# Linear attention: head sums of the diagonal products taken with the products as the moving side on four column blocks, then transposed

## The chip, the cores and the metric

The kernel runs on one core of one Trainium2 chip. The metric is the time of one execution in microseconds of device time. TensorE (PE) multiplies, with its weight loads shown apart as PEld; VectorE (DVE), ScalarE (ACT) and GpSimd (POOL) work elementwise; SyncE (SP) issues the DMAs. Each engine runs its own instructions in the order in which the program lists them.

## The reference

Two layers over 2048 latent tokens and 256 context tokens. Each layer normalises and modulates the stream, projects it once, runs three branches (a gated delta rule, a neighbourhood attention, and a gated linear attention, "GLA"), gates them and projects back. The change lies in GLA alone. Per direction, with `g` the running sum of the gates inside a chunk, it computes

```python
diff = bcum[..., :, None, :] - bcum[..., None, :, :]
decay = jnp.where(tril, jnp.exp(jnp.where(tril, diff, 0.0)), 0.0)
amat = jnp.einsum('bhnid,bhnjd,bhnijd->bhnij', q, k, decay)
o_intra = jnp.einsum('bhnij,bhnjv->bhniv', amat, v)
```

for 4 heads of 32 key channels, then adds the part that comes from the state of earlier chunks. Both directions are summed.

## The kernel before

All 2304 tokens are cut into 6 blocks of 384 tokens (`BLK`), each 3 tiles of 128 tokens (`TPB`). `Dense.run` multiplies the stream by a group of projection columns, block by block: for each output, 24 matmuls of line 197 (8 slices of the model width, 3 products of a high and a low part each). After the dense work of block `b` of the first such run of a layer, the program calls `Gla.block(b)` (`after=gla.block`). So twice per run of the kernel, once per layer, there is a stretch in which TensorE has dense work and GLA work side by side. There are 12 GLA blocks; in the first block of the second layer only one tile of three needs scores (`i0 = 2`), so they count as 11.33 full ones.

`Gla.block` holds channels on the partitions (128 = 4 heads x 32) and tokens along the free side. VectorE forms the running sums `B` (lines 432 and 433), and for seven levels `s` = 64, 32, 16, 8, 4, 2, 1 the decayed keys and queries `a` (lines 444 to 449, with ScalarE's exponential on line 448); the last ones of these are what the diagonal products need. GpSimd then multiplies keys and queries elementwise into `qkp` (line 472): four products x = 0 to 3, one for the token with itself and three for its near neighbours. A sum over the 32 channels of each head is a sum over partitions, so TensorE does it: for each product and each tile one matmul with the 128x128 product as the stationary side and 4 columns of a constant (`mats[:, 8]`) as the moving side, into `pD` (line 476). VectorE copies `pD` to `dg` (line 478). `scores` (once per head) multiplies keys and queries of the levels 64 to 4 on small tiles of the array, into `pA` and `pB` (lines 494 and 501); ScalarE copies `pA` to `A` (line 504); VectorE builds `G` from `pB` and `dg` (lines 507 to 511) and puts it into `A` (line 514). `chunk` multiplies `A` with the values (`pO`, line 528), transposes the keys (`pk`, line 537) and forms the change of the state (`pS`, line 543).

All these PSUM tiles (`pr`, `pg`, `pD`, `pA`, `pB`, `pO`, `pk`, `pS`) rotate through 4 buffers of one tag, in the order in which the program allots them. `qkp` x = 1 to 3 lies in the SBUF buffers of tag `rp`, `B` in those of tag `B`. Which ready instruction stands next on an engine is decided when the program is built, by a scheduler that estimates times and prefers what stands earlier in the program; on the chip the order is then fixed.

Of the kernel before, what the change touches and what calls it, by code (L numbers as in the profile page):

```python
# [11 lines left out]
F32 = mybir.dt.float32  # L12
# [15 lines left out]
BLK = 384  # L28
NB = T // BLK
TPB = BLK // 128  # L30
# [305 lines left out]
class Gla:  # L336
# [64 lines left out]
    def block(self, b):  # L401
        e, nc, P = self.e, self.e.nc, self.p
        mats = e.mats
# [27 lines left out]
        B = P.tile([128, 2, BLK], F32, tag="B", name="B")  # L431
# [3 lines left out]
        i0 = max(0, self.first - b * TPB)  # L435
        o = i0 * 128
# [31 lines left out]
        qkp = []  # L468
        for i, (l, r) in enumerate([(qk[:, 0], qk[:, 1])] + [(KQ[s][:, 0], KQ[s][:, 1]) for s in (1, 2, 2)]):
            if i % 2 == 0:  # L470
                qkp.append(P.tile([128, 2, BLK], F32, tag="rp" if i else "ga", name="qkp"))
            nc.gpsimd.tensor_tensor(quad(qkp[-1][:, i % 2]), quad(l), flip(quad(r), i), op=ALU.mult)
        pD = self.ps.tile([128, TPB, 4, 4], F32, tag="ps", name="pD")
        for x in range(4):
            for i in range(i0, TPB):
                nc.tensor.matmul(pD[:, i, x], qkp[x // 2][:, x % 2, i * 128:i * 128 + 128], mats[:, 8, 4 * min(x, 1):4 * min(x, 1) + 4], start=True, stop=True)  # L476
        self.dg = P.tile([128, TPB, 4, 4], F32, tag="dg", name="dg")
        nc.vector.tensor_copy(self.dg[:, i0:], pD[:, i0:])
        A = [self.scores(h, KQ, i0) for h in range(4)]
        for i in range(TPB):  # L480
            self.chunk(b * TPB + i, i, A, E, et[:, i:i + 1], V[:, i])
# [1071 lines left out]
```

## Time and profile before

| what | value |
|---|---|
| median of 3 runs | 3960.82 us (3921.74 to 3962.12) |
| profiled execution | 3949.59 us, its span 3947.8 us |
| TensorE busy | 3618.4 us, 92% |
| VectorE busy | 2455.6 us, 62% |
| ScalarE busy | 1687.4 us, 43% |
| TensorE's mean granted clock | 0.91 |

The span is the time from the first to the last instruction of the profiled execution. Busy times of the engines overlap. A row of a timeline gives the start in us from the span's start, the length in us, the engine, the line, the operation, the tile that is written and those that are read, the shape, and in brackets the idle time of the engine before it and what ended it. A float32 matmul leaves two records (x272 is 136 matmuls). The granted clock has two levels in these rows: 0.5 is 1.2 GHz, 1.0 is 2.4 GHz.

### The profile page before, as it was taken

What the parts mean: (1) busy time and instruction counts of PE and PEld (TensorE: products, weight loads), DVE (VectorE), ACT (ScalarE), POOL (GpSimd) and SP (SyncE); (2) the same over time, 40 slices, a digit from 0 to 9 for tenths busy, and PEclk for the clock granted to TensorE, in tenths of its full rate; (3) what the DMA queues carried; (4) which work ended last, traced back from release to release, by engine and by line L of the source; (5) the groups of instructions that cost most, each with busy time, mean ns of one, the idle gap of its engine ahead of it and who ended that gap; (6) DMA issues with size and microseconds to landing.
All of it is one profiled execution on the core that took longest, in us unless ns stands there. A gap on an engine that the chain in (4) does not pass through costs nothing.

```text
span 3947.8 us, 76664 instructions
## 1 busy us (share of the span) xinstructions
PE 3618.4 (92%) x27262; PEld 3113.5 (79%) x27262; DVE 2455.6 (62%) x6983; ACT 1687.4 (43%) x4587; POOL 682.8 (17%) x1118
## 2 busy tenths in 40 slices
PE   6999999999989999998998999999999899989898
PEld 3787778769977888896776778777899688878787
DVE  4456463668966477446884655427788567653577
ACT  3533233435533455565544333333455235545531
POOL 0221111220102222220002211102102132222100
PEclk8988889999999799999997889899999888879899
DMA  9844325886687777766755444468665977685664
GB/s 294 284 133 141 124 84 167 264 264 198 208 271 227 223 210 208 211 204 213 238 178 172 141 129 137 131 202 246 202 213 193 324 207 213 194 215 171 218 204 125
DMA packets 756085, 787.55 MB, mean 199 GB/s; under 512 B 190206, under 2 KB 665206, under 8 KB 755702
## 3 DMA queue, kind: packets, MB, share of 16 engines
q1 hardware_dynamic: 755702, 782.64, 64.5%
q8 instruction: 216, 3.54, 0.4%
q14 instruction: 167, 1.37, 0.1%
HBM read 548.41 MB, written 234.03 MB: 198 GB/s over the span
## 4 chain that ended last, share of the span: by engine, by line
PE 60%; DMA 18%; DVE 13%; ACT 4%; SPq 2%; issue 2%; POOL 1%; DVEq 0%; ACTq 0%; POOLq 0%
PE p L197 29%; PE py L197 6%; DMA mm<-MS 3%; PE p L1258 3%; DMA gb<-GR 2%; DMA o<-OA 1%; PE pv L1022 1%; PE po L1042 1%; PE pd L1029 1%; DMA kk<-KK 1%; PE p L104 1%; PE pk L1011 1%; PE po L1044 1%; DVE acc L661 1%; PE pD L476 1%
## 5 line engine op out<-in xcount | busy, mean ns | idle before, releaser
L197 PE MATMUL p<-mm,wh 128*128 128x384 f32 (+1 forms) x3648 | 995.8, 352 | 51.9 <-DMA mm<-MS 32.4
L197 PEld LDWEIGHTS p<-mm,wh 128*128 128x128 f32 (+1 forms) x3648 | 661.3, 191 | 123.2 <-DMA mm<-MS 48.1
L197 PE MATMUL p<-mm,wl 128*128 128x384 f32 (+1 forms) x1824 | 630.0, 347 | 0.4 <-DVE wl L189 0.3
L197 PE MATMUL p<-wh,mm 128*128 128x512 f32 (+1 forms) x1696 | 566.5, 407 | 11.4 <-DMA mm<-MS 4.5
L197 PEld LDWEIGHTS p<-wh,mm 128*128 128x128 f32 x1696 | 329.4, 197 | 89.7 <-DMA mm<-MS 9.2
L661 DVE SCALAR_TENSOR_TENSOR acc<-pre,cw,acc 128x384 f32<-128x384 f32 (+1 forms) x576 | 358.3, 640 | 49.8 <-ACT acc L659 43.0
L197 PEld LDWEIGHTS p<-mm,wl 128*128 128x128 f32 (+1 forms) x1824 | 346.5, 190 | 16.1 <-issue 9.7
L197 PE MATMUL p<-wl,mm 128*128 128x512 f32 (+1 forms) x848 | 342.4, 404 | 1.2 <-DVE rst L395 1.0
L197 PEld LDWEIGHTS p<-wl,mm 128*128 128x128 f32 x848 | 167.3, 197 | 36.2 <-issue 2.2
L197 PE MATMUL py<-w,mh 128*128 128x512 f32 x544 | 178.8, 407 | 7.7 <-ACT mh L1380 5.0
L1004 POOL TENSOR_TENSOR kd<-kk,eD 128x256 f32<-128x256 f32 x144 | 89.3, 620 | 453.2 <-DMA kk<-KK 190.0
L1274 DVE SCALAR_TENSOR_TENSOR zt<-zt,p 128x256 f32<-128x256 f32 (+1 forms) x102 | 51.5, 507 | 178.9 <-ACT zt L1273 177.9
L1237 ACT ACTIVATE w<-w,mn 128x696 f32<-128x696 f32 (+2 forms) x136 | 112.8, 830 | 82.8 <-DVE mn L1234 80.0
L651 POOL COPY pre<-pre 128x4 f32<-128x4 f32 x120 | 81.0, 678 | 383.8 <-DVE acc L661 190.9
L925 DVE TENSOR_TENSOR tmp<-M 96x30 f32<-96x30 f32 (+4 forms) x360 | 126.6, 352 | 29.7 <-issue 21.9
L1015 DVE SCALAR_TENSOR_TENSOR R<-pk,neG,kk 128x128 f32<-128x128 f32 x272 | 81.4, 344 | 100.9 <-PE pk L1011 100.0
L865 DVE SCALAR_TENSOR_TENSOR gb<-gb,Gt,mats 128x128 f32<-128x128 f32 x288 | 86.4, 359 | 91.4 <-DMA gb<-GR 88.9
L1258 PE MATMUL p<-v,wl 120*128 120x64 f32 (+1 forms) x960 | 140.5, 285 | 0.0
L926 DVE TENSOR_TENSOR M<-M,tmp 96x30 f32<-96x30 f32 (+4 forms) x360 | 127.3, 354 | 6.3
L1258 PEld LDWEIGHTS p<-v,wl 120*128 120x128 f32 (+1 forms) x960 | 130.6, 204 | 0.7
L186 ACT CAST wh<-raw 128x512 fp32r<-128x512 f32 (+3 forms) x144 | 75.8, 555 | 123.6 <-DMA raw<-in_w_in 105.7
L189 POOL TENSOR_TENSOR mm<-mm 128x384 fp32r<-128x384 f32 x48 | 58.4, 1222 | 398.2 <-ACT mm L186 391.7
(307 smaller groups left out, 8136.1 us busy)
## 6 DMA issues: line engine op xcount, KB each, us to landing
mm<-MS SPq DMA_DIRECT2D x384, 384.0 KB
kk<-KK SPq DMA_DIRECT2D x144, 512.0 KB
MS<-mm SPq DMA_DIRECT2D x96, 384.0 KB
raw<-in_w_in SPq DMA_DIRECT2D x104, 256.0 KB
w<-in_w_mod SPq DMA_DIRECT2D x96, 256.0 KB
M<-m SPq DMA_DIRECT2D x36, 512.0 KB
mm<-M SPq DMA_DIRECT2D x96, 192.0 KB
KK<-kq SPq DMA_DIRECT2D x96, 192.0 KB
```

The source lines that it names most:

```text
L186: eng_hi.copy(hi, src)
L189: eng_lo.tensor_tensor(lo, src, hi.bitcast(F32), op=ALU.subtract)
L197: e.nc.tensor.matmul(p, x(k), y(k), start=n == 0, stop=n == 3 * KD - 1)
L651: nc.gpsimd.tensor_copy(pre[:, 0:4], pre[:, m:m + 4])
L661: nc.vector.scalar_tensor_tensor(acc[:, :n], pre[:, k:k + n], w(kind, k), acc[:, :n], op0=ALU.mult, op1=ALU.add)
L865: nc.vector.scalar_tensor_tensor(E[:, d, h], gb[:, d, h], self.G[:, d, c, h0 + h:h0 + h + 1], e.mats[:, 1 + d], op0=ALU.subtract, op1=ALU.min)
L925: nc.vector.tensor_tensor(tv, col, row, op=ALU.mult)
L926: nc.vector.tensor_tensor(o, o, tv, op=ALU.add)
L1004: nc.gpsimd.tensor_tensor(kd, kv[:, :, 0], self.eD[:, d, c, h0:h0 + 2].unsqueeze(2).to_broadcast([128, 2, 128]), op=ALU.mult)
L1015: nc.vector.scalar_tensor_tensor(R[:, h], pk[:, h], sc(self.neG, h), kv[:, h, 1], op0=ALU.mult, op1=ALU.add)
L1237: nc.scalar.activation(w[:, a, 0:256 + nk], w[:, a, 0:256 + nk], AF.Exp, bias=m[:, a:a + 1], scale=-1.0, accum_out=sm[:, a:a + 1])
L1258: nc.tensor.matmul(p[:, a], l, r, start=j == 0, stop=j == len(parts) - 1)
```

## The change

The four products are no longer the stationary side. The constant, widened to 32 columns of which the first 4 count, is stationary, and the product of a whole block (384 tokens) is the moving side. Each of the four matmuls writes its own 32 partitions of one PSUM tile `pX`, that is, its own block of 32 columns of the array (`tile_position=(0, 32 * x)`). The result has heads on the partitions and tokens along the free side; ScalarE copies it to `dT` (in the SBUF buffer of tag `B`), TensorE transposes `dT` tile by tile into `pD`, which is now 3 x 128 wide, and VectorE copies the 4 columns that count of each 32 to `dg`.

```diff
-        pD = self.ps.tile([128, TPB, 4, 4], F32, tag="ps", name="pD")
+        pX = self.ps.tile([128, BLK], F32, tag="ps", name="pX")
         for x in range(4):
-            for i in range(i0, TPB):
-                nc.tensor.matmul(pD[:, i, x], qkp[x // 2][:, x % 2, i * 128:i * 128 + 128], mats[:, 8, 4 * min(x, 1):4 * min(x, 1) + 4], start=True, stop=True)
+            c = 4 * min(x, 1)
+            nc.tensor.matmul(pX[32 * x:32 * x + 32, o:], mats[:, 8, c:c + 32], qkp[x // 2][:, x % 2, o:], start=True, stop=True, tile_position=(0, 32 * x))
+        dT = P.tile([128, 2, BLK], F32, tag="B", name="dT")[:, 0]
+        nc.scalar.copy(dT[:, o:], pX[:, o:])
+        pD = self.ps.tile([128, TPB, 128], F32, tag="ps", name="pD")
+        for i in range(i0, TPB):
+            nc.tensor.transpose(pD[:, i], dT[:, i * 128:i * 128 + 128], e.ident)
         self.dg = P.tile([128, TPB, 4, 4], F32, tag="dg", name="dg")
-        nc.vector.tensor_copy(self.dg[:, i0:], pD[:, i0:])
+        nc.vector.tensor_copy(self.dg[:, i0:], pD[:, i0:].rearrange("p i (x c) -> p i x c", x=4)[:, :, :, 0:4])
```

Since six lines are added, what was line 494 is line 500 after the change, 501 is 507, 504 is 510. The new lines are 477 (`pX`), 479 (`dT`), 482 (the transposes) and 484 (`dg`).

The order of the instructions changes with it. TensorE before, second block of the first layer, from the middle of the scores: `pD` x9 are the last nine of the twelve sums, `pA` and `pB` the scores.

```order
L501 MATMUL pB<-a 32x32 x40
L494 MATMUL pA<-a 64x64 x2
L494 MATMUL pA<-a 32x32 x4
L501 MATMUL pA<-a 32x32 x4
L494 MATMUL pA<-a 64x64 x2
L494 MATMUL pA<-a 32x32 x4
L501 MATMUL pA<-a 32x32
L476 MATMUL pD<-mats,qkp 128x4 x9
L501 MATMUL pB<-a 32x32 x8
L501 MATMUL pA<-a 32x32 x3
```

Of that block's 216 score matmuls 125 stand ahead of these nine sums and 91 behind them. TensorE after the change, the same block, first at the last three of the four new sums and then at the transposes:

```order
L197 MATMUL p<-mm,wh 128x384
L197 MATMUL p<-mm,wl 128x384
L477 MATMUL pX<-qkp,mats 32x384 x3
L371 MATMUL pt<-ident,r_4563 128x48 x3
L197 MATMUL p<-mm,wh 128x384 x2
L197 MATMUL p<-mm,wl 128x384
```

```order
L197 MATMUL p<-wh,mm 128x512
L197 MATMUL p<-wl,mm 128x512
L197 MATMUL p<-wh,mm 128x512 x2
L482 MATMUL pD<-ident,dT 128x128 x3
L500 MATMUL pA<-a 64x64 x2
L500 MATMUL pA<-a 32x32 x4
L507 MATMUL pA<-a 32x32 x4
L507 MATMUL pB<-a 32x32 x8
```

All 216 score matmuls now stand behind the transposes, in one run without dense work between them. This is so in each of the 12 blocks (in the short one 72, with 4 dense matmuls among them); between the last `pX` and the transposes 12 to 28 dense matmuls stand. Before, 76 to 138 of the 216 stood ahead of the last sums.

VectorE after the change, fourth block of the first layer, from the copy to `dg` on:

```order
L1087 SCALAR_TENSOR_TENSOR nqk<-p,nqk 128x192 x2
L484 COPY dg<-pD 128x48
L513 COPY G<-pB 128x96
L515 COPY_PREDICATED G<-masks,pB 128x96
L517 COPY_PREDICATED G<-masks,dg 128x96 x4
L520 COPY_PREDICATED A<-masks,G 32x3x32 x4
L513 COPY G<-pB 128x96
L515 COPY_PREDICATED G<-masks,pB 128x96
```

Before, the first two operations (`G<-pB`) of two heads stood ahead of the copy to `dg` in this block; now those of all four heads stand behind it.

## Rows read from the trace of the kernel before

**Rows 1.** Page of the profile: span; then busy time and share of each engine.

```profile
span 3947.8 us, 76664 instructions
PE 3618.4 (92%) x27262; PEld 3113.5 (79%) x27262; DVE 2455.6 (62%) x6983; ACT 1687.4 (43%) x4587; POOL 682.8 (17%) x1118
```

**Rows 2.** Page, the chain that ended last: shares of the span by line.

```profile
PE p L197 29%; PE py L197 6%; DMA mm<-MS 3%; PE p L1258 3%; DMA gb<-GR 2%; DMA o<-OA 1%; PE pv L1022 1%; PE po L1042 1%; PE pd L1029 1%; DMA kk<-KK 1%; PE p L104 1%; PE pk L1011 1%; PE po L1044 1%; DVE acc L661 1%; PE pD L476 1%
```

**Rows 3.** Busy by stretch: length, PE, PEld, DVE, ACT, POOL, PEclk, DMA.

```profile
92.00:690.00 598.00, 555.20 (x5161) 465.82 (x5160) 300.94 (x769) 217.36 (x535) 97.27 (x85) 0.87 0.49 158
2068.00:2600.00 532.00, 481.43 (x4542) 398.87 (x4542) 275.95 (x742) 187.55 (x451) 97.06 (x82) 0.85 0.46 147
```

**Rows 4.** Groups, line 476: busy, mean ns of one | idle before, releaser.

```profile
L476 PE MATMUL pD<-mats,qkp 128*128 128x4 f32 x272 | 47.4, 303 | 19.8 <-POOL qkp L472 19.6
```

**Rows 5.** Timeline, two blocks, lines 476 and 478: start, length, instruction, idle before.

```profile
369.30 4.00 PE L476 MATMUL pD<-mats,qkp 128*128 128x4 f32 x18 [3.04 <-POOL qkp L472]
373.34 0.21 DVE L478 COPY dg<-pD 128x48 f32<-128x48 f32 x1 [3.89 <-PE pD L476]
...
2426.94 2.24 PE L476 MATMUL pD<-mats,qkp 128*128 128x4 f32 x18 [0.32 <-POOL qkp L472]
```

**Rows 6.** Timeline: four column blocks (pS), 384 moving columns (pr), two transposes (pk).

```profile
330.08 0.43 PE L543 MATMUL pS<-v,kd 128*32 128x64 f32 x16
330.44 1.56 PE L417 MATMUL pr<-qk,mats 128*128 128x384 f32 x4
331.93 0.91 PE L425 MATMUL pg<-rc,w2p 32*128 32x384 f32 x2
...
391.19 0.39 PE L537 MATMUL pk<-ident,E 128*128 128x128 f32 x2
391.34 0.42 PE L197 MATMUL p<-mm,wh 128*128 128x384 f32 x1
```

**Rows 7.** Groups of instructions: the scores of lines 494 and 501.

```profile
L494 PE MATMUL pA<-a 32*32 32x32 f32 (+1 forms) x1632 | 94.6, 256 | 19.7 <-DVE a L449 19.2 <-ACT A L504 0.4
L501 PE MATMUL pB<-a 32*32 32x32 f32 x2176 | 49.2, 227 | 2.5 <-issue 1.6 <-DVE a L449 0.7
L501 PE MATMUL pA<-a 32*32 32x32 f32 x1088 | 42.6, 224 | 6.9 <-DVE a L449 6.6 <-issue 0.3
```

**Rows 8.** Timeline: score groups of one head and token tile, at both clock levels.

```profile
2429.11 0.52 PE L494 MATMUL pA<-a 32*64 32x64 f32 x12
2429.75 0.52 PE L494 MATMUL pA<-a 32*64 32x64 f32 x12
...
2431.31 0.74 PE L494 MATMUL pA<-a 32*64 32x64 f32 x12
2432.29 0.74 PE L494 MATMUL pA<-a 32*64 32x64 f32 x12
```

**Rows 9.** Dense matmuls (line 197) in the 17 half-clock stretches: first, last, sum.

```profile
205.00:228.90 23.90, 10.04 (x28) 8.87 (x29) 0.50 0.11 31
...
2488.50:2515.90 27.40, 4.66 (x14) 4.22 (x14) 0.50 0.14 43
sum 266.30, PE 79.56 PEld 67.63; mean PE 4.68 PEld 3.98
```

**Rows 10.** Timeline of VectorE: one head from its G to the next head's G.

```profile
378.64 0.26 DVE L507 COPY G<-pB 128x96 f32<-128x96 f32 x1
...
380.45 1.09 DVE L514 COPY_PREDICATED A<-masks,G 32x96 f32<-32x96 int32 x4
381.57 0.26 DVE L507 COPY G<-pB 128x96 f32<-128x96 f32 x1
```

**Rows 11.** Groups of instructions: matmuls that read the scores A, line 528.

```profile
L528 PE MATMUL pO<-v,A 128*128 128x64 f32 x272 | 44.3, 298 | 7.7 <-DVE A L514 7.6
```

**Rows 12.** Groups by form: ScalarE's copy of a 128x384 score tile.

```profile
L504 ACT COPY A<-pA 128x384 f32<-128x384 f32 x44 | 21.0, 476 | 145.1 <-PE pA L501 145.0
```

**Rows 13.** Timeline of weight loads: first small tile behind a dense run.

```profile
2356.41 0.41 PEld L494 LDWEIGHTS pA<-a 32*64 32x64 f32 x12 [0.35 <-issue]
```

## The prediction

> **What bounds the kernel now.** I read the page first: the span is 3947.8 us and TensorE is busy for 92% of it [rows 1]. In the chain that ended last the dense matmuls of line 197 hold 29%, and line 476, the line that is changed, still has 1% of its own [rows 2], some 40 us. So the kernel is bound by TensorE, and what TensorE does in the two stretches with GLA blocks should show in the time.
>
> Second, the stretches. From 92 to 690 us and from 2068 to 2600 us TensorE is busy for 555.2 of 598 us and 481.4 of 532 us, VectorE for 300.9 and 276.0 us, ScalarE and GpSimd for less [rows 3]. The reader should see two things. TensorE, 93% and 90% busy, has hardly any slack, and behind each GLA block there is dense work of the next one, so TensorE time that is freed is used. And the granted clock is 0.87 and 0.85, lower than the 0.91 of the whole run: part of the work there goes at 1.2 GHz.
>
> Third, the changed line. Its 272 records (136 matmuls) keep TensorE busy for 47.4 us, and TensorE idles another 19.8 us in front of them, for GpSimd's products [rows 4]. The timeline shows why four moving columns cost so much: 18 records take 4.00 us at the low clock and 2.24 us at the high one, 222 and 124 ns each, which is the time of loading a 128x128 product as weights; VectorE sits idle for 3.89 us until they end [rows 5].
>
> **The sums themselves.** I count 11.33 full blocks. Now a block costs 47.4 / 11.33 = 4.2 us. After the change there are four matmuls of 384 moving columns in float32. The same shape on full columns is `pr`: its two matmuls (4 records) go from 330.44 us to the next start at 331.93 us, 0.75 us each [rows 6]. The first product is ready early and runs alone: 0.75 us. The other three are issued together on three column blocks. Whether they overlap is shown by `pS`, whose tiles are 128x32 on four column blocks: 8 matmuls of 64 columns take 0.36 us to the next start, while by `pr` one after the other they would take 8 x 0.75 x 64 / 384 = 1.0 us, a factor of 2.8 [rows 6]. Three products then cost 3 x 0.75 / 2.8 = 0.8 us; without overlap 2.25 us. The transposes go by `pk`: two have 0.15 us to the next start and a length of 0.39 us [rows 6]; I put three at 0.5 us. The sum is 2.05 us with overlap and 3.5 us without. I take the overlap, since `pS` is the same tile shape: 4.2 - 2.05 = 2.15 us less per block, 24 us in all. The other end is 0.7 us x 11.33 = 8 us.
>
> The crossings between a full array and small tiles also cost: the first small weight load behind a dense run waits 0.35 us for nothing else that the profile shows [rows 13]. The new sums stand apart from the scores, at two places, so a block gets four more crossings; by this row they take back 4 x 0.35 x 11.33 = 16 us. But the scores, which the order shows broken into several runs now, come in one run afterwards and save crossings. I take zero for the balance, with 16 us as the bad end. The Trainium skill has a rule that speaks against this change: by "TensorEngine Tiling (Array Packing)", section Tiling Modes, a switch of the tiling mode drains TensorE. By that rule alone the sum would lose the 16 us; by the row and the order together it loses nothing.
>
> ScalarE gets 12 copies of 0.48 us, by its copy of a 128x384 score tile [rows 12], 5 us on an engine that is less than half busy [rows 1]. The order puts 12 to 28 dense matmuls between the last sum and the transposes, and a dense matmul takes 10.04 / 28 = 0.36 us at half clock [rows 9], so 0.18 us at full; 2 us or more cover the copy. Without that cover TensorE would wait for the 0.48 us in each block, 5 us.
>
> **The scores, which move.** The order shows all scores behind the transposes. I read that from the buffers: `pD` is allotted ahead of the first `pA`, and now it is first written by the transposes. What this gives: TensorE now stops in front of the scores for levels that VectorE has not finished, 19.2, 6.6 and 0.7 us on the three groups, 26.5 us together [rows 7]. After the change the levels must be done before the last sums, so these waits go, and dense work stands in their place. The wait for GpSimd in front of the last sums (19.6 us, rows of the same group as above [rows 4]) stays. I take 20 of the 26.5 us, since part of the dense work that steps in waits for its own loads; the ends are 0 and 26.5.
>
> **The clock.** In the 17 stretches at half clock around the scores, 266.3 us together, dense matmuls are busy for 79.6 us [rows 9]. At full clock these would take half, 40 us less. Before, dense work lies among the scores at the low clock; after, most of it lies ahead of them, and only what follows the scores meets the low clock. I take 12 of the 40 us, with 0 and 40 as ends. The scores keep their own price: the group of one head and tile takes 0.64 us at full and 0.98 us at half clock [rows 8].
>
> **What is late next.** One run of 12 such groups takes 7.7 to 11.8 us. VectorE needs 2.93 us per head, from `G` to the next `G` [rows 10], and starts when the first head's three groups are done, 1.9 to 2.9 us after the transposes. The third head is ready 10.7 to 11.8 us after them. TensorE comes to its first `pO` of that head after the run and about 1 us of other work, at 8.7 to 12.8 us. So it waits 0 to 3 us there. Now this wait is 7.6 us in all [rows 11]. I take 1.5 us per block, 17 us, so 10 us more; the ends are 8 us less and 26 us more.
>
> **The sum.** Minus 24, minus 20, minus 12, plus 10: 46 us less. The profiled execution took 3949.6 us, 0.3% below the median of the runs shown, 3960.8. That gives 3904 us. With all the good ends (24, 26.5, 40 and 8 less) it is 3851 us; with the bad ones (8 and 16 for the sums, no gain on waits and clock, 26 us more) 3984 us. The scheduler also reorders work outside the two stretches. I have no row for what that does and leave room for it in the range.
>
> **The rivals.**
> *The waits only move: 3936 us.* TensorE waits as long for something else ahead of the scores (loads, or GpSimd's products), and the low clock lasts as long as now. For it speaks that the products' wait is untouched [rows 4]. Against it, dense work is available. Then 24 - 10 = 14 us are left.
> *The column blocks do not pay: 3920 us.* The three sums run one behind the other, or the crossings are charged in full: 16 us of the 46 are lost. Against it speaks `pS` [rows 6].
> *More than I take: 3869 us.* The good ends of waits and clock hold together, 26.5 and 30 us, with the 24 us and no new wait at `pO`.
> *Slower: 4010 us.* VectorE's work on the scores, all behind the transposes now, is in front of TensorE in every block. Four heads are 11.7 us of it, and where weight splits or evacuations of dense work stand among them it is more. If TensorE waits at the third head's `pO` for 10.8 us in each block in place of 1.5, the time is 3904 + 9.3 x 11.33 = 4010 us. It decides from 4000 us on, about 10 us of wait. For it speaks that `G` of two heads was partly built ahead of `dg`, and is not any more. Against it, the run of scores itself takes nearly as long as VectorE needs [rows 8, 10], and VectorE is busy for only half of the stretches [rows 3]. The Trainium skill, same page, section Performance Considerations, warns of this side: tiling speeds up TensorE but not the emptying of PSUM.
>
> **How the numbers follow.** My forecast around 3904 us has 0.45, the moved waits 0.25, more gain 0.14, column blocks that do not pay 0.08, slower 0.08. The predicted time is 3904 us. The range reaches from 3860 us, which takes in most of the larger gain, to 3968 us, which takes in the moved waits with some 30 us for reordering; the slower case and the far ends stay out. Two measurements of this kernel can be told apart by about 1%, that is 39.6 us of 3960.8. Faster by more than that is under 3921 us: most of the forecast (0.38), the larger gain (0.14) and half of the column case (0.04), 0.56. Slower, over 4000 us: 0.08. Within 1%: 0.36.
>
> **What would show it.** Right: the records of the new sums and transposes together keep TensorE busy for about 23 us in place of 47; the three late sums overlap instead of standing 0.75 us apart; no idle time in front of the scores that ends with VectorE's levels; the mean clock of the two stretches rises by a few hundredths. Wrong: the transposes wait for ScalarE, `pO` waits for VectorE for more than 3 us per block, the half-clock stretches get longer than 23.5 us per block (266.3 / 11.33), or the difference lies outside the two stretches, where nothing was meant to change.

## The result, and the profile after

The changed kernel takes 3978.02 us (median of 16 runs, 3961.91 to 3992.50), the kernel before 3942.14 us on the same chip (16 runs): a ratio of 1.0101, 95% interval 1.0078 to 1.0124. It is 36 us slower by the medians and some 40 us by the ratio, where 46 us less were predicted, and it lies above the range. The profiled execution took 3990.42 us. Medians and ratios in this document leave out slow runs, those more than 1.5% above the fastest of the same kernel.

The page, its first lines, as [rows 1] of before:

```profile
span 3988.6 us, 76462 instructions
PE 3612.9 (91%) x27120; PEld 3078.3 (77%) x27120; DVE 2456.7 (62%) x6983; ACT 1699.1 (43%) x4599; POOL 675.5 (17%) x1118
```

TensorE is busy 5.5 us less, and the span is 41 us longer. So the time went into waiting. The groups of instructions say what became of the terms that the prediction costed. Columns: busy us, mean ns of one, then idle time in front and what ended it.

```profile
L500 PE MATMUL pA<-a 32*32 32x32 f32 (+1 forms) x1632 | 87.5, 247 | 1.5 <-issue 1.5
L507 PE MATMUL pB<-a 32*32 32x32 f32 x2176 | 53.4, 218 | 15.2 <-issue 14.9 <-DVE dg L484 0.2
L534 PE MATMUL pO<-v,A 128*128 128x64 f32 x272 | 42.6, 300 | 0.1
L507 PE MATMUL pA<-a 32*32 32x32 f32 x1088 | 39.9, 216 | 6.5 <-issue 6.5
...
L477 PE MATMUL pX<-qkp,mats 128*32 128x384 f32 (+1 forms) x96 | 20.8, 527 | 27.1 <-POOL qkp L472 27.0
...
L482 PE MATMUL pD<-ident,dT 128*128 128x128 f32 x34 | 5.7, 272 | 0.0
```

The new sums and the transposes keep TensorE busy for 26.5 us (20.8 and 5.7), the old sums did so for 47.4 us [rows 4]. The waits of the scores for VectorE's levels, 26.5 us [rows 7], are gone, and the wait at `pO` [rows 11] has not grown but fallen from 7.7 to 0.1 us. But 22.9 us of "issue" (TensorE idles and waits for nothing that the page shows) are new in front of the scores: 1.5, 14.9 and 6.5 us on the three groups, where it was 1.9 us. So the idle time in front of the scores falls only from 29.1 to 23.2 us. The wait for GpSimd's products is 27.1 us in place of 19.8 [rows 4].

Where the waiting lies is seen by stretch. I take the first from 92 us to the last matmul of line 682 in the first layer (688 after the change), which belongs to the convolution that follows the GLA work; the second from the first rope product of the second layer (line 418) to the last matmul of that line there. First before, then after; columns as in [rows 3].

```profile
92.00:1137.00 1045.00, 988.22 (x7458) 836.25 (x7456) 643.19 (x1812) 417.16 (x1075) 173.28 (x207) 0.92 0.61 191
2083.00:3075.00 992.00, 920.90 (x6929) 802.76 (x6927) 612.87 (x1756) 381.69 (x978) 172.31 (x204) 0.91 0.57 180
sum 2037.00, PE 1909.12 PEld 1639.02 DVE 1256.06 ACT 798.85 POOL 345.59; mean PE 954.56 PEld 819.51 DVE 628.03 ACT 399.43 POOL 172.80
```

```profile
92.00:1163.00 1071.00, 969.39 (x7343) 803.61 (x7342) 641.90 (x1797) 419.84 (x1079) 174.90 (x207) 0.91 0.59 184
2115.00:3108.00 993.00, 905.60 (x6878) 781.33 (x6876) 608.30 (x1764) 388.61 (x987) 163.10 (x204) 0.92 0.58 182
sum 2064.00, PE 1874.98 PEld 1584.95 DVE 1250.20 ACT 808.45 POOL 338.00; mean PE 937.49 PEld 792.47 DVE 625.10 ACT 404.22 POOL 169.00
```

TensorE has 34 us less to do in the two stretches (1909.1 to 1875.0), and they take 27 us more: its idle time goes from 128 to 189 us. The 26 us are lost in the first layer; the second stays at 992 to 993 us although 15 us of work left it: its idle time grows as much. (The other 14 us of the 41 lie outside. There the profiles of all kernels below differ by some 50 us, and two profiles of one kernel by 31, so I read nothing from that part.)

The first layer is explained by the period of the GLA blocks. VectorE's rope product (line 418) has two records per block; its rows, before and after, give the first and the last start in the six blocks of that layer.

```profile
L418 DVE TENSOR_TENSOR qk<-pr,rp x12: 557/558/558, 174.4 to 563.4; 128x384 f32<-128x384 f32 x12
```

```profile
L418 DVE TENSOR_TENSOR qk<-pr,rp x12: 548/557/558, 170.4 to 599.8; 128x384 f32<-128x384 f32 x12
```

With 0.6 us between the two records of a block, five periods are 388.4 us before and 428.8 us after: 77.7 and 85.8 us a block. Where the 8.1 us come from is seen in the timeline of the fourth block. Before:

```profile
409.94 1.20 DVE L418 TENSOR_TENSOR qk<-pr,rp 128x384 f32<-128x384 f32 x2 [0.32 <-PE pr L417]
...
437.33 4.35 POOL L472 TENSOR_TENSOR qkp<-a 128x384 f32<-128x384 f32 x3 [14.03 <-DVE etr L461]
441.74 4.00 PE L476 MATMUL pD<-mats,qkp 128*128 128x4 f32 x18 [0.62 <-POOL qkp L472]
445.78 0.21 DVE L478 COPY dg<-pD 128x48 f32<-128x48 f32 x1 [2.36 <-PE pD L476]
451.25 0.42 PE L501 MATMUL pB<-a 32*32 32x32 f32 x16
483.77 0.43 PE L543 MATMUL pS<-v,kd 128*32 128x64 f32 x16
485.08 1.20 DVE L418 TENSOR_TENSOR qk<-pr,rp 128x384 f32<-128x384 f32 x2 [0.32 <-PE pr L417]
```

After:

```profile
429.73 1.20 DVE L418 TENSOR_TENSOR qk<-pr,rp 128x384 f32<-128x384 f32 x2 [0.32 <-PE pr L417]
...
457.48 4.98 POOL L472 TENSOR_TENSOR qkp<-a 128x384 f32<-128x384 f32 x3 [13.90 <-DVE a L449]
462.52 1.50 PE L477 MATMUL pX<-qkp,mats 128*32 128x384 f32 x6 [7.35 <-POOL qkp L472]
464.16 0.48 ACT L479 COPY dT<-pX 128x384 f32<-128x384 f32 x1 [5.25 <-PE pX L477]
469.70 0.49 PE L482 MATMUL pD<-ident,dT 128*128 128x128 f32 x3
470.23 0.21 DVE L484 COPY dg<-pD 128x48 f32<-128x48 f32 x1 [8.09 <-PE pD L482]
476.32 0.43 PE L507 MATMUL pB<-a 32*32 32x32 f32 x15 [1.04 <-issue]
...
480.28 0.42 PE L507 MATMUL pB<-a 32*32 32x32 f32 x16
512.49 0.43 PE L549 MATMUL pS<-v,kd 128*32 128x64 f32 x16
513.80 1.20 DVE L418 TENSOR_TENSOR qk<-pr,rp 128x384 f32<-128x384 f32 x2 [0.32 <-PE pr L417]
```

From the last product on GpSimd to `dg` it is 4.1 us before (441.68 to 445.78) and 7.8 us after, since 5.7 us of dense work stand between the sums and the transposes. The last of the scores ends 10.0 us after that product before and 18.2 us after the change: before, half of them were done while GpSimd made its products; now the whole run of 11 us follows `dg`. From there to the last `pS` it is 32 us both times, and the next block's rope begins 1 us behind that. The chain of a block is serial, and the change put the scores into it.

The row at 476.32 us shows one of the pauses that the groups above call "issue". There are 19 of them in the 12 runs of scores, of 0.3 to 3.3 us; the kernel before has two. In the first five blocks of the first layer they come to 11.8 us, 2.3 of the 8.1 us a block, and in the second layer to 11.0 us, which takes up most of the 15 us of work that left it. The last section says what the trace shows beside them.

Dense work that stands in front of a waiting block is used up that much earlier. So `reverse`, the pass over the chunks in the other direction that follows the six blocks (line 567, 573 after the change), is nearly bare in the first layer after the change; before, dense work stood between its matmuls. The stretch from the last `pS` to the last matmul of `reverse`, before and after (length, PE busy, ..., granted clock):

```profile
637.00:692.00 55.00, 51.62 (x247) 45.85 (x247) 15.38 (x45) 26.01 (x142) 10.29 (x16) 0.97 0.67 206
```

```profile
677.00:717.00 40.00, 19.14 (x50) 8.23 (x38) 13.68 (x38) 21.51 (x111) 10.70 (x28) 0.54 0.66 210
```

Behind it TensorE waits for the weights of the next run as well:

```profile
736.38 1.01 PE L197 MATMUL p<-mm,wh 128*128 128x384 f32 x2 [19.52 <-ACT wh L186]
```

### The profile page after: what moved, and what is told of

Same layout as the page of the kernel before. It is cut to its first block, busy times and chain, and to the rows that moved or that the text cites. A ratio compares the mean times of both kernels' runs of the same rounds, so it can differ in the third digit from the quotient of the medians.

```text
span 3988.6 us, 76462 instructions
## 1 busy us (share of the span) xinstructions
PE 3612.9 (91%) x27120; PEld 3078.3 (77%) x27120; DVE 2456.7 (62%) x6983; ACT 1699.1 (43%) x4599; POOL 675.5 (17%) x1118
## 4 chain that ended last, share of the span: by engine, by line
PE 63%; DMA 17%; DVE 9%; ACT 4%; issue 3%; SPq 2%; POOL 1%; DVEq 0%; ACTq 0%; POOLq 0%
PE p L197 28%; PE py L197 7%; PE p L1264 3%; DMA mm<-MS 3%; PE pA L500 2%; PE p L104 2%; DMA gb<-GR 2%; DMA raw<-in_w_in 2%; PE pv L1028 1%; PE pd L1035 1%; PE po L1048 1%; PE pk L1017 1%; PE pt L1255 1%; DVE a L449 1%; DMA kq<-KK 1%
## 5 line engine op out<-in xcount | busy, mean ns | idle before, releaser
L197 PEld LDWEIGHTS p<-mm,wh 128*128 128x128 f32 (+1 forms) x3648 | 665.7, 192 | 168.4 <-issue 51.6
L871 DVE SCALAR_TENSOR_TENSOR gb<-gb,Gt,mats 128x128 f32<-128x128 f32 x288 | 89.1, 367 | 84.2 <-DMA gb<-GR 84.2
L1031 ACT ACTIVATE v<-pv,Wt 128x128 f32<-128x128 f32 x288 | 88.7, 364 | 98.3 <-PE pv L1028 97.6
L1048 PE MATMUL po<-v,A 128*128 128x128 f32 x544 | 117.8, 302 | 12.1 <-DVE S L1040 8.7
```

Of the source, the lines that this page charges most:

```text
L197: e.nc.tensor.matmul(p, x(k), y(k), start=n == 0, stop=n == 3 * KD - 1)
L871: nc.vector.scalar_tensor_tensor(E[:, d, h], gb[:, d, h], self.G[:, d, c, h0 + h:h0 + h + 1], e.mats[:, 1 + d], op0=ALU.subtract, op1=ALU.min)
L1031: nc.scalar.activation(v[:, h], pv[:, h], AF.Copy, scale=sc(self.W, h))
L1048: nc.tensor.matmul(po[:, h], A[:, h], v[:, h], start=True, stop=not n)
```

## The experiments

The theories at the start: A, the scores behind the transposes lengthen the chain of each block, dense work runs out, and the end of the first layer's stretch comes later; B, the new sums cost more than the old ones; C, any new order of instructions scatters by about 1%. Every ratio is to the kernel before on the same chip, with its 95% interval. "Early" and "late" say where the scores stand: partly ahead of the sums as in the kernel before, or all behind them. "Stretches" is the sum of the two stretches above, one profile each; a profiled execution can lie up to 28 us off the median of its kernel (g6), so differences of some 20 us between two kernels there are not safe.

| kernel | sums, scores | ratio | stretches, of it TensorE busy | period, layer 0 | last `reverse` matmul / line 682, layer 0 |
|---|---|---|---|---|---|
| before | old, early | 1 | 2037, 1909 | 77.7 | 692 / 1137 |
| after | new, late | 1.0101 [1.0078, 1.0124] | 2064, 1875 | 85.8 | 717 / 1163 |
| e1 | new, early | 1.0023 [0.9992, 1.0053] | 2027, 1876 | 77.2 | 685 / 1133 |
| e2 | old, late | 1.0083 [1.0051, 1.0114] | 2045, 1880 | 80.6 | 709 / 1159 |
| e3 | as after, GLA first | 1.0057 [1.0028, 1.0085] | 2052, 1869 | 84.2 | 713 / 1161 |
| e5 | as e1, GLA first | 1.0002 [0.9970, 1.0035] | 2011, 1874 | 74.5 | 672 / 1122 |
| e9 | none, early | 0.9957 [0.9924, 0.9990] | 1992, 1850 | 74.9 | 672 / 1126 |
| g1 | old, early, front apart | 1.0104 [1.0070, 1.0139] | 2060, 1901 | 58.9 | 611 / 1157 |
| g2 | new, late, front apart | 0.9983 [0.9949, 1.0018] | 2030, 1876 | 58.6 | 613 / 1134 |
| g3 | new, early, front apart | 1.0031 [1.0001, 1.0062] | 2049, 1894 | 57.1 | 613 / 1157 |
| g5 | as g1, `bd` on VectorE | 1.0034 [0.9997, 1.0071] | 2050, 1905 | 56.0 | 600 / 1143 |
| g6, g9 | as g3, `bd` on VectorE | 1.0033 [0.9999, 1.0067], 1.0012 [0.9983, 1.0040] | 2007, 1878 and 2005, 1874 | 53.6, 54.3 | 584 / 1125, 589 / 1128 |
| g8 | old, late, both edits | 1.0068 [1.0040, 1.0096] | 2031, 1885 | 56.4 | 604 / 1139 |
| g4, g7 | as g2, `bd` on VectorE | 0.9899 [0.9843, 0.9956], 0.9931 [0.9902, 0.9960] | 1999, 1869 and 1998, 1865 | 56.8, 56.5 | 606 / 1129, 600 / 1126 |

### Sums and scores apart: e1 and e2

In e1 the new sums and the transposes share one PSUM tile. Its buffer is first written by the sum of x = 0, as in the kernel before, and the scores stand early again:

```diff
-        pX = self.ps.tile([128, BLK], F32, tag="ps", name="pX")
+        pX = self.ps.tile([128, TPB, 128], F32, tag="ps", name="pX")
+        pD, pX = pX, pX.rearrange("p i t -> p (i t)")
...
-        pD = self.ps.tile([128, TPB, 128], F32, tag="ps", name="pD")
```

> The new sums stay, but the transposes write back into the PSUM buffer of the sums, so that no second buffer is allotted ahead of the scores; in the order some 70 to 140 of the 216 scores of a block stand ahead of the transposes again, and the reverse pass has dense work between its steps. Theory A (the scores that were pushed behind the transposes lengthen each GLA block, dense work runs out before GLA ends, and the end of the first layer's stretch lies bare): 3915 to 3945 us, ratio 0.993 to 1.001 of before, with the block periods back near 77 us from about 85. Theory B (the new sums themselves cost: column blocks, the extra copy, the transposes): as slow as the change, 3965 to 3990 us. Theory C (any new order scatters by about 1%): anywhere between 3930 and 3990, without a link to the block period.

e2 is the kernel before with one tile more that is first written late, which moves nearly all scores behind the sums (at most 4 of the 216 of a block still stand ahead). VectorE then copies `dg` in two pieces:

```diff
+        pZ = self.ps.tile([128, TPB, 4], F32, tag="ps", name="pZ")
...
-                nc.tensor.matmul(pD[:, i, x], ...
+                nc.tensor.matmul(pD[:, i, x] if x < 3 else pZ[:, i], ...
```

> The kernel before with its old sums; only the sums of the last product go to a PSUM tile of their own, allotted ahead of the scores and written late, and one more small copy on VectorE is needed. In the order nearly all scores then stand behind the sums, as in the change. Theory A: slower than before by 20 to 40 us, 3960 to 3985 us, if the late scores are the cause by themselves; less if the end of the stretch keeps dense work (in this order the reverse pass is still mixed with dense work): then 3940 to 3960. Theory B: as before, 3935 to 3950 us. Theory C: anywhere.

e1: 3943.86 us beside 3935.92, 1.0023. e2: 3972.89 us, 1.0083. So the late scores cost 0.8%, some 33 us, by themselves, with the old sums, and the new sums with early scores cost nothing that is clear of the noise. But they gain nothing either, though TensorE is busy for 33 us less. (Busy time is not work alone: in e2 it falls by 29 us with the old sums, which take 35.1 us there in place of 47.4 now that they stand behind dense work.) For the first layer the period says why: 77.2 us in e1.

```profile
L418 DVE TENSOR_TENSOR qk<-pr,rp x12: 556/556/558, 171.0 to 557.8; 128x384 f32<-128x384 f32 x12
```

The chain of a block is as long as before: the three late sums are cheaper, and the copy to `dT` and the transposes are new. That these two balance is argued, not measured apart.

### GLA work ahead of dense work: e3 and e5

```diff
             if after:
-                after(b)
+                with e.tc.high_priority(PRI // 2):
+                    after(b)
```

The same edit on the changed kernel (e3) and on e1 (e5).

> The change, with the GLA blocks given to the scheduler at higher priority than the dense work. The scores still stand behind the transposes, but the first layer's reverse pass is not one lump of 17 matmuls any more. Theory A, tail part: the bare end of the first layer (15.8 us of waits in the reverse pass and 19.5 us for weights) shrinks, 3940 to 3965 us. Theory B: 3970 to 3985 us. Theory C: anywhere.

> One PSUM buffer for the sums and the transposes, and GLA blocks at higher priority. Theory A: the best of the four, 3905 to 3940 us, since the blocks are short and the end is covered. Theory B: 3965 to 3990 us. Theory C: anywhere.

e3: 3962.26 us beside 3935.92, 1.0057. The period fell only from 85.8 to 84.2 us, and the first layer ends where it did; in the two stretches 12 us are gained. e5: 3944.89 us, 1.0002; its stretches are 26 us shorter than those of the kernel before, but its profiled execution was 19 us faster than its median, so this is no gain that the runs show. Both ratios lie some 0.2 to 0.4% below those of the kernels without the edit. A higher place in the order doesn't take the scores out of the chain.

### What the sums are worth at most: e9

```diff
-        pD = self.ps.tile([128, TPB, 4, 4], F32, tag="ps", name="pD")
-        for x in range(4):
-            for i in range(i0, TPB):
-                nc.tensor.matmul(pD[:, i, x], ...
...
-        nc.vector.tensor_copy(self.dg[:, i0:], pD[:, i0:])
+        for x in range(4):
+            nc.vector.tensor_copy(self.dg[:, i0:, x], qkp[x // 2][:, x % 2, o:].rearrange("p (i t) -> p i t", t=128)[:, :, 0:4])
```

> The kernel before without the head sums on TensorE: dg is filled with some elements of the products by four small VectorE copies, so GpSimd's products still stand in the chain, but the 136 matmuls of line 476 (47.4 us of TensorE, and 19.8 us of idle time in front of them) are gone. This is more than any form of the sums can save. Theory P: the time falls by 47 to 67 us, 1.2 to 1.7%. Theory D: in the first layer only the chain counts, and it gets shorter by the three late sums, about 3 us a block, 15 us over the five blocks; in the second layer about half of 22 us comes back; 20 to 30 us, 0.5 to 0.8%.

This kernel leaves the head sums out and fills `dg` with single elements of the products. 3915.54 us beside 3931.57, 0.9957: some 17 us by the ratio, with an interval from 4 to 30. That is far from 47 to 67 us; the interval takes in the 20 to 30 us of the other theory. The total hides two different layers. The first layer's stretch in e9, the stage between the two, and the second layer's:

```profile
92.00:1126.00 1034.00, 958.65 (x7292) 808.99 (x7290) 643.53 (x1814) 415.88 (x1071) 169.26 (x207) 0.92 0.61 191
1126.00:2099.00 973.00, 875.45 (x6582) 763.95 (x6583) 613.88 (x1764) 477.90 (x1356) 170.90 (x353) 0.91 0.70 210
2099.00:3057.00 958.00, 891.77 (x6802) 770.46 (x6801) 619.93 (x1775) 381.65 (x981) 169.23 (x204) 0.93 0.60 187
```

In the first layer TensorE has 30 us less to do than before, and 11 us come back. In the second it has 29 us less, and 34 us come back: there TensorE does set the time. The stage between, where the edit alters no line, is 27 us longer than before (946 us) in this profile; why is open. It takes back more than half of the 45 us that the two layers gain. In the first layer the last `reverse` matmul comes some 20 us earlier, 14 of them by the five periods, which are 2.8 us shorter each.

The table's last column makes this a rule of this kernel's first layer. In the seven kernels from before to e9 the periods differ by 11 us and `reverse` ends anywhere from 672 to 717 us, but line 682 ends 445 to 455 us behind it in all of them. There the end of `reverse` goes with the end of the stretch, and the chain of blocks with the end of `reverse`. In the second layer this does not hold: after the change the last `reverse` matmul ends 558 us behind the first rope product in place of 516, and the stretch is as long as before.

### The wait for weights behind reverse: f1, f2, f3

In the changed kernel and in e1 the weights of the next run queue on SP behind loads that can wait. Here they are put first, in e1 (f1), in the kernel before (f2, the control) and in the changed kernel (f3):

```diff
-                nc.sync.dma_start(r, self.w4[:, k:k + step, c0:c0 + cw])
+                with e.tc.high_priority(self.pri):
+                    nc.sync.dma_start(r, self.w4[:, k:k + step, c0:c0 + cw])
...
+                            dn.pri = PRI // 2
                             dn.run(W, gdn.conv(P, psh, 0) + gdn.conv(P, psh, 1), [], bufs=6, raws=4)
+                            dn.pri = 0
```

> The new sums with pX and pD in one PSUM buffer, and in addition the weight loads of the run that follows the GLA stretch (first half of the convolution's columns) stand at the head of SP's queue as soon as their buffers are free, ahead of the small loads of the gates and tables and of w_mod. Theory D: in the first layer the time is set by a chain: last GLA block, reverse, then these weights, then the dense work that needs them. In the one-buffer kernel TensorE idles 17.1 us there for the first cast of these weights, which starts 16 us after the last reverse matmul; in the kernel before it is 4 us. With the loads first, the cast should start 4 to 6 us after it, the wait should fall below 6 us, the convolution's transposes should start about 80 us after the end of reverse in place of 92, and the time should be about 12 us below that of the one-buffer kernel, 0.3% (a ratio of about 0.999 to the kernel before). Theory P: TensorE's amount of work sets the time, and the wait only moves: ratio as the one-buffer kernel, 1.002.

> The kernel before with the same move of the weight loads alone. Here the first cast comes 4 us after the last reverse matmul already, and TensorE has dense work left until 713 us. Both theories: 0 to 3 us less, a ratio of 0.999 to 1.000. It is the control for the other two: if this gains 12 us as well, the gain has nothing to do with the exposed tail.

> The changed kernel with the same move of the weight loads alone. Here TensorE idles 19.5 us for the first cast, which starts 19 us after the last reverse matmul. Theory D: the wait falls below 6 us and the time by 12 to 15 us, to a ratio of about 1.006 from 1.010; the rest of the loss, the GLA blocks that end 40 us later, stays. Theory P: 1.010 as before.

f1: 1.0002 [0.9969, 1.0036]; f2: 1.0032 [1.0003, 1.0060]; f3: 1.0114 [1.0066, 1.0161]. f3, where 1.006 was expected, is a miss; the interval of f1 takes in both theories. The wait did get shorter, in f3 from 19.5 us to

```profile
729.12 1.01 PE L197 MATMUL p<-mm,wh 128*128 128x384 f32 x2 [12.48 <-ACT wh L186]
```

and in f1 from 17.1 to 9.0 us, but line 682 still ends 447 us behind `reverse` in both. What was won was waited for a little later. By these runs the exposed wait is a sign that TensorE has run out of work, not the cost. The control f2 also says what theory C is worth: with nothing but loads moved, the time went up by 0.3%, so ratios that differ by no more than that are not read as a gain or a loss.

### The chain off the path: g1, g2, g3

The rope and the gates of a block use `pr` and `pg`, which queue in the ring of four PSUM buffers behind the last `pS` of the block before. Here they come from another PSUM pool of the kernel (`psh`, handed to the object as `self.pf`):

```diff
-            pr = self.ps.tile([128, BLK], F32, tag="ps", name="pr")
+            pr = self.pf.tile([128, BLK], F32, tag="dn", name="pr")
...
-            pg = self.ps.tile([128, BLK], F32, tag="ps", name="pg")
+            pg = self.pf.tile([128, BLK], F32, tag="dn", name="pg")
```

> The kernel before, with the four PSUM tiles of the front of a GLA block (pr, pr, pg, pg) taken from another PSUM pool of two buffers that stands idle here, in place of the ring of four that the rest of the block uses. So the rope and the gates of the next block no longer queue behind the last pS of the block before. Nothing else is changed. Theory D: the first layer's stretch is set by the chain of GLA blocks (77.7 us a block from rope to rope), and TensorE idles 47.6 us there because of it. The period should fall to 60 to 70 us, reverse end at 640 to 670 us in place of 692, the dense work last until after it, and the time fall by 15 to 35 us: ratio 0.991 to 0.996. Theory P (TensorE's work alone sets the time): no change, 0.998 to 1.002.

> The changed kernel with the front of a block in the other PSUM pool, as in the kernel above. The scores still stand behind the transposes, all 216 of them. Theory D: late scores cost only through the chain, so with the chain off the path they cost nothing, and the new sums' 21 to 24 us of TensorE come to show: 10 to 24 us below the kernel before with the same edit, ratio 0.986 to 0.993 to the kernel before. If the late scores cost something by themselves (theory L), it stays 25 to 40 us above the one-buffer kernel with the same edit.

> The new sums with pX and pD in one PSUM buffer (part of the scores ahead of the transposes) and the front of a block in the other PSUM pool. Theory D: as the changed kernel with this edit, within 0.3% of it, and 10 to 24 us below the kernel before with this edit, ratio 0.986 to 0.993. If the new sums save no time even where TensorE is the bound, it equals the kernel before with this edit.

In all three the period falls to 57 to 59 us, `reverse` ends 72 to 104 us earlier than without the edit, and the 445 us behind it no longer hold: dense work is left when the blocks are done. But g1 is slower, 3979.86 us beside 3938.89, where 15 to 35 us less were expected. g2 takes 3929.49 us: with the chain off the path the changed kernel loses its 1%, and it is 50 us below g1. So with the new sums the late scores cost time through the chain, and not through the pauses in their runs as such: g2 has 25.4 us of these and loses nothing, e2 has 7.6 us and loses 0.8%. Late scores even do better than early ones here: g3, with the same sums, takes 3958.47 us, 0.5% above g2, where at most 0.3% was expected to part them.

In g1 there is a new wait. TensorE waits 26.1 us at `pO` for `bd`, the product of state and head mask on GpSimd, which takes 51.6 us for 33 in place of 21.3. One of the long ones, with the first of the VectorE rows beside it, the last one, and who waits:

```profile
294.88 0.34 DVE L447 TENSOR_TENSOR a<-B 128x192 f32<-128x192 f32 x1
294.90 9.23 POOL L525 TENSOR_TENSOR bd<-S,mats 128x256 f32<-128x256 f32 x1 [3.83 <-DVE S L547]
...
300.98 2.68 DVE L449 TENSOR_TENSOR a<-a,qk 128x768 f32<-128x768 f32 x3
304.19 1.22 PE L526 MATMUL pO<-bd,E 128*128 128x256 f32 x2 [7.12 <-POOL bd L525]
```

`bd` needs 0.61 us when nothing hinders it. Here VectorE works through the next block's level differences without a pause until 303.66 us, and `bd` ends at 304.13 us. Overlapping the blocks made the two meet. This does not settle the miss: g2 and g3 wait as long for `bd`, 22.2 and 27.1 us, and are faster than g1. What else g1 loses by is open.

### The best kernel, and old and new sums beside each other: g4 to g9

`bd` of `chunk` made on VectorE:

```diff
-                nc.gpsimd.tensor_tensor(bd, self.S[0].unsqueeze(1) ...
+                nc.vector.tensor_tensor(bd, self.S[0].unsqueeze(1) ...
```

> The changed kernel with the front of a block in the other PSUM pool, and in addition the small product bd of chunk (state times head mask, 128x256) made on VectorE in place of GpSimd. In the kernels with the front moved, bd on GpSimd takes up to 9 or 12 us in place of 0.61 us, each time while VectorE runs the level differences of the next block back to back; TensorE waits 11.4 us in the first stretch and 10.7 us in the second for it. Theory G: GpSimd is held off while VectorE works that way; on VectorE itself bd takes its turn, the waits for bd fall below 5 us together, and the time falls by 10 to 20 us, to a ratio of 0.993 to 0.996 (from 0.998 without this edit). Rival V: on VectorE bd queues behind the same level differences, and TensorE waits as long there: 0.997 to 1.001.

> The kernel before (old sums, part of the scores ahead of them) with the front of a block in the other PSUM pool and bd of chunk on VectorE: the best kernel so far without the change. Theory D (the change's sums save TensorE 21 to 24 us, and this shows where TensorE and not the chain of blocks sets the time; late scores cost nothing there): 20 to 30 us above the changed kernel with the same two edits (0.990), a ratio of 0.995 to 0.998. Rival E (the two edits alone made the gain, the sums are worth nothing anywhere): 0.988 to 0.992.

> The new sums with pX and pD in one PSUM buffer, so that part of the scores stands ahead of the transposes, with the same two edits. It differs from the best kernel (0.990) only in where the scores stand. Theory D: off the path of the chain it doesn't matter, a ratio of 0.988 to 0.993. If scores that stand ahead cost TensorE waits for VectorE's levels, which late scores don't have: 10 to 25 us more, 0.993 to 0.997.

> The changed kernel with the same two edits once more, on the same chip as the two others, so that the three can be compared: 0.990 again, 0.984 to 0.995.

> The old sums with x = 3 in a PSUM tile of its own (so all scores stand behind the sums, in both layers), with the front of a block in the other PSUM pool and bd on VectorE. It completes the square: old or new sums, scores early or late, all with the same two edits. So far: old and early 1.003, new and early 1.003, new and late 0.993 (0.990 in an earlier call). Theory S: it is the late scores alone that make the gain, and the sums are worth nothing: 0.990 to 0.996. Theory B: only both together make it, since the new sums take dense work between themselves and the transposes: 1.000 to 1.005. If the sums are worth their 24 us only where the scores are late: 0.998 to 1.000.

> New sums and early scores with the two edits once more, beside the other one on the same chip, and for a second profile: the first one was 30 us shorter than the median of its runs. 1.003 again, 0.999 to 1.007; idle and low-clock time of TensorE in the two GLA stretches above those of the changed kernel with the same edits.

g4, the changed kernel with both edits, takes 3890.35 us beside 3933.57, and again 3902.89 us beside 3934.69 (g7): 0.7 to 1.0% below the kernel before and 1.7 to 2.0% below the changed one. It beats both. On the same chip as g7 the old sums with the same edits take 3945.29 us (g5). So here, with the chain off the path, the change is worth 42 us. (The old sums gain nothing from that: g5 is no faster than the kernel before, so the chain was not the only limit there.) The sums of the stretches, g5 and then g7:

```profile
sum 2050.00, PE 1905.48 PEld 1633.51 DVE 1266.74 ACT 800.83 POOL 315.68; mean PE 952.74 PEld 816.75 DVE 633.37 ACT 400.41 POOL 157.84
```

```profile
sum 1998.00, PE 1865.01 PEld 1588.32 DVE 1260.28 ACT 806.30 POOL 304.33; mean PE 932.50 PEld 794.16 DVE 630.14 ACT 403.15 POOL 152.17
```

52 us less, of it 40 us of TensorE's busy time and 12 us of idle time. The profiled execution of g5 was 21 us slower than its median, so 52 us are rather too much. Of the 40 us the sums are 21 (38.7 to 17.6 us); the granted clock, 0.92 and 0.91 in the two stretches of g5, is 0.93 in both of g7. In the idle time one wait goes that the change was not meant to touch, the one for `bd`, which is now made on VectorE (5.8 and 6.1 us in g6 and g9, 1.2 us in g8). g5, then g7:

```profile
L526 PE MATMUL pO<-bd,E 128*128 128x256 f32 x66 | 27.2, 501 | 18.8 <-DVE bd L525 18.8
```

```profile
L532 PE MATMUL pO<-bd,E 128*128 128x256 f32 x66 | 26.1, 483 | 0.6 <-DVE bd L531 0.6
```

How the 42 us divide is not settled. In the stretches the new sums save 44 us with early scores (2050 to 2006, the mean of g6 and g9) and 33 us with late ones (2031 to 1998, g8 to g7); late scores save 19 us with the old sums and 8 us with the new ones. By the whole times late scores with the old sums are 0.3% slower (1.0068 for g8, above all that was expected, and 1.0034 for g5, intervals that overlap), and new sums with early scores no faster (g6, where 0.988 to 0.997 was expected, and g9): only the two together show a gain. In g9, whose profiled execution took its median time, what the stretches gained is lost in the stage between them, where the change alters no line. That stage in g7 and in g9, columns as above:

```profile
1126.00:2064.00 938.00, 853.81 (x6564) 746.49 (x6563) 611.97 (x1747) 476.06 (x1351) 169.79 (x353) 0.93 0.71 217
```

```profile
1128.00:2100.00 972.00, 879.38 (x6558) 769.05 (x6558) 607.52 (x1742) 474.57 (x1347) 170.96 (x353) 0.90 0.69 209
```

Nearly the same number of matmuls is busy for 26 us more at a granted clock of 0.90 in place of 0.93. Why the low level of the clock is granted for longer there is open; the scheduler's order differs a little in that stage too, and no run separates the two.

## Why the prediction was wrong

**The step that failed** is in its second paragraph: "behind each GLA block there is dense work of the next one, so TensorE time that is freed is used". A busy share of 93% was read as proof that TensorE sets the time. In the second layer that holds: without the sums (e9) 34 us come back for 29 us of work. In the first layer it does not: 11 us come back for 30, since the chain of blocks ends there when the dense work is all but used up, and what lengthens the chain lengthens the stretch. So the terms of the sum were hardly a gain in the first layer, and the length of the chain, the term that counted, stood nowhere in it.

**The scores, which move.** "These waits go, and dense work stands in their place" came true in its first half only: the 26.5 us are gone, but 22.9 us of pauses inside the runs of scores are there, so the term of 20 us was worth 6 us. For this term the rival of the waits that only move was near the truth. And the step asked only what TensorE does meanwhile, not what the block does. The scores had run while GpSimd made its products; moved behind `dg` they lengthen each block. The last score now ends 18.2 us after the last product in place of 10.0, and the period is 8.1 us longer. Five periods give 40 us; dense work that had stood between the matmuls of `reverse` was gone by then, which shortens `reverse` itself from 55 to 40 us, and 25 us remain at its end, 26 us at the end of the stretch. The rows for it were there: `pr`, the front of the next block, follows directly on the last `pS` in [rows 6], and six such pairs in the timeline give the period.

**What is late next.** The term of plus 10 us for `pO` had the wrong sign, 7.7 to 0.1 us, and the slower rival, 4010 us, named the wrong place: VectorE was never in front of TensorE there. It had the right side for a wrong reason, which is luck.

**The sums themselves** were sized well: 21 us less of TensorE's busy time, where 24 were taken. But 12 of these 21 us come with the place and not with the form, since the old sums take 35.1 us in e2. The three late sums overlap fully, 0.78 us to the next start at full clock in 8 of 11 full blocks (0.8 predicted), one alone 0.76 us, the transposes 0.42 us (0.5 predicted): 1.96 us a block where 2.05 were taken. The rule of the Trainium skill, "TensorEngine Tiling (Array Packing)", section Tiling Modes, by which the 16 us for crossings would be lost, got nothing in the sum. No run shows such a drain apart from the rest, and none shows that it costs nothing.

**The cover of the copy** is there, but it is no gift: the 5.7 us of dense work between sums and transposes in the block above, which hide ScalarE's 0.48 us, stand in the chain of the block.

**The clock.** The low-clock stretches around the scores come to 225 us in place of 266 [rows 9], so a block has 19.9 us of them and not 23.5; but the bare `reverse` and what follows it add one of 61 us (680 to 742 us). In the stretches of [rows 3] the mean clock rises from 0.87 and 0.85 to 0.89 and 0.86, about as was predicted; over the whole stretches above it does not: 0.92 and 0.91 before, 0.91 and 0.92 after.

**The total**, minus 46 us, is near the minus 42 us measured between g5 and g7, but that is luck. Of its terms only the sums are found there, at 21 us. g5 waits for VectorE's levels in front of the scores for only 1.5 us, so the term of 20 us had nothing to remove; the 18 us of waiting for `bd` that go instead stood nowhere in the sum.

## What to carry to other kernels

Before freed time of an engine is priced, find what ends the stretch: lay the period of the serial chain beside the work that fills it, and ask what is left to do when the chain ends. A busy share of 93% does not tell the two apart; leaving the work out altogether (e9) does, if it is read stage by stage and not by the total. When an edit changes where instructions stand, follow the moved ones through the chain of their own block as well as through the queue of their engine. Buffers that rotate in the order of allotment move work that the edit doesn't name, and giving the front of a block its own buffers took the chain off the path here.

## What the runs showed of the hardware

A GpSimd product of 128x256 that takes 0.61 us took 9.23 us beside VectorE's two-operand work: it ended 0.5 us behind a whole run of back-to-back VectorE instructions, not behind one. The Trainium skill, "SBUF — State Buffer", section Who interferes with whom, says that a VectorE instruction with two inputs in SBUF contends with a GpSimd instruction that reads SBUF, and calls the port pair that they share an exclusive lock. The trace agrees on the pair, but the block here lasts from 294.90 to 304.13 us, over some twenty VectorE instructions of 0.34 to 0.94 us each. Moved to VectorE, where `bd` has a median of 0.41 us, the product saved the changed kernel with its front apart another 0.5 to 0.8% (g2 to g7 and g4, on different chips).

Three float32 matmuls of 384 moving columns on three column blocks of 32 take as long to the next start, 0.78 us, as one alone, 0.76 us (full granted clock, 8 of 11 full blocks).

The 19 pauses in the runs of scores go with the supply of instructions. The page after the change has, among the DMA queues (packets, MB, share):

```profile
q8 instruction: 215, 3.52, 0.4%
```

That is one packet of 16 KB for some 250 of the 54,240 matmul and weight load records of TensorE. By the trace's records of that queue each of the 19 pauses ends 1.3 to 1.6 us after such a packet has landed; the pauses in the scores of all the other kernels here do so too, at 1.1 to 1.6 us. So TensorE seems to have waited there for its next instructions: a run of 216 score matmuls has 864 such records in some 11 us. No run changes the supply, so the cause is inferred and not shown.
